# Merging the inverse blocks of a gated DeltaNet: products of four quadrants interleaved in PE's queue

## The chip, the cores and the metric

The kernel runs on one core of one Trainium2 chip. The metric is the device time of one execution in microseconds. The median of three runs shown of the kernel before is 1520.39 us (1517.37 to 1524.07).

## The reference, cut to what matters

One layer of a hybrid backbone: 256 context tokens and 1024 latent tokens of width 1024 pass a modulated RMSNorm, one wide input projection, two parallel groups of heads (a bidirectional gated DeltaNet with four heads of 128, and a bidirectional retention with rotary positions), an output projection, and a SwiGLU. All inputs and the output are float32. The change lies in the gated DeltaNet, in the triangular solve:

```python
kb = kc * bc[..., None]
A = jnp.where(strict, jnp.einsum('nbhid,nbhjd->nbhij', kb, kc) * decay, 0.0)
...
sol = lax.linalg.triangular_solve(A + jnp.eye(CHUNK, dtype=A.dtype), rhs,
                                  left_side=True, lower=True, unit_diagonal=True)
```

For every chunk, head and direction a unit triangular matrix I + A has to be inverted. The kernel works with chunks of 128 tokens, ten for the 1280 tokens, so there are 10 x 4 units for each of two directions. In the forward direction the stored (transposed) matrix is triangular one way, in the backward direction the other way.

## The kernel before, in words

**Where the time stands.** The kernel computes the modulated input `hhi`, `hlo` (each float32 value split in two halves for fast products), projects it group by group (`token_major`, `conv_block`), prepares and inverts the DeltaNet blocks (`pre`, `invert`, `merge`), scans both directions (`step`), runs the retention beside the scan (`backward`, `forward`), and ends with output projection and feed-forward part.

**The inverse.** `invert(b)` takes a batch of chunks (batches of four, four and two: 16, 16 and 8 units for each direction) and inverts the 32 x 32 diagonal blocks by forward substitution on DVE (lines 638 and 640, 31 steps of two operations). `merge(b)` builds the 128 x 128 inverses from them. It loads the matrices into `U` (one tile, [128, direction, chunk, head, 128]) and writes the inverted diagonal blocks over their places; `t64` holds the transposed inverted blocks. Both have one buffer, so the next batch's loads wait for the merge before to be done with them.

A merge has two levels. For a block-triangular matrix with diagonal inverses X and Y and off-diagonal block C, the off-diagonal block of the inverse is -X C Y. On the first level the blocks are 32 x 32, and there are four such places: two directions `d` times two halves `p`. Each place uses one quadrant `a` of 32 partitions and its neighbour `bb`; for direction 0 these are (0, 1) and (2, 3), for direction 1 they are (1, 0) and (3, 2). Before the change the code walks d, then p, and for each place:

- L679: for all units, a product with quadrant `a` as rows, into the partitions of `bb` of a PSUM bank;
- L681: DVE negates these 32 partitions into `xt1`;
- L683: for all units, the second product, rows `bb`, into the partitions of `a` of the same bank;
- L685: ACT copies them into `U`;
- L688 and L690, for p equal to d only: a third product, the transposed form that the second level needs, and its copy into `t64`.

On the second level the blocks are 64 x 64. For each direction, and for each group of eight units: L701 (product), L702 (negation of 64 partitions into `xt2`), L704 (second product), L705 (copy into `U`). L707 then writes each chunk of `U` to DRAM for the scan. Every product here is a float32 product, which the profile shows as two passes, each with a weight load of its own.

**PSUM.** `bank_b` draws from three banks of the tag `pb`. `pre` uses them too (`kk`, `qt`, `kq`), as do the scan steps of direction 0. The projections (`tm`) have three banks of their own, `pa`.

**What sets the order.** A planner goes through the program with a cost model, and issues at each point the instruction that is ready and stands earliest in the program, engine by engine; each engine then runs its queue in the planned order. So while a merge waits for DVE or ACT, the planner fills PE with products of later projections. In the stretch in question these are the groups of `token_major` that follow in the program: 8 and 9, then two scan steps for each direction, then 2 to 5 with rotary finish (`fin_rope`: DVE at L398 and L401, GpSimd at L403, the store at L391 from one of two `res` buffers). Their products are L381, L382 and L383; their weights are loaded and split by ACT (L319) and DVE (L320). When the projections are done, their memory goes to the retention, which then runs beside the remaining scan steps.

Of the kernel before, what the change touches and what calls it, by code (L numbers as in the profile page):

```python
# [17 lines left out]
P = 128  # L18
# [19 lines left out]
def build(nc, tc, ap, dbg=None, stop=None, marks=None):  # L38
    root = ExitStack()
    V, S, G, T, SY = nc.vector, nc.scalar, nc.gpsimd, nc.tensor, nc.sync  # L40

    def pool(name, bufs=1, side=None, space=None):
        kw = {}
        if side is not None:
            kw["side"] = side
        if space is not None:
            kw["space"] = space
        if space is not DRAM:
            kw["reuse_waits"] = "tile"
        es = ExitStack()  # L50
        p = es.enter_context(tc.tile_pool(name=name, bufs=bufs, **kw))
        root.push(es)
        p_close[id(p)] = es
        return p
# [10 lines left out]
    def checkpoint(name):  # L65
        if dbg is not None:
            marks.append((name, int(nc.cur_bb.bb.instructions[-1].name.split("-")[-1])))
        if stop == name:
            raise Stop()
# [16 lines left out]
    def bank(tag, name):  # L86
        return PS["pool"].tile([P, 512], F32, tag=tag, name=name, bufs=PS["tags"][tag])
# [4 lines left out]
    def bank_b(name):  # L92
        return bank("pb", name)
# [67 lines left out]
    try:  # L161
# [44 lines left out]
        for k in range(KT):  # L206
            for i in range(2):
                w = PA.tile([P, 1024], F32, tag="adaw", name="adaw", bufs=7)
# [3 lines left out]
                if k > last:  # L212

                    for j in range(8):
                        T.matmul(pst[:, 64 + 2 * j:66 + 2 * j], w[:, j * P:(j + 1) * P], csl[:, k, :],
                                 start=True, stop=True)
                    rows_of(0)
                    continue
                if 2 * k + i in PLAIN:

                    for j in range(2):
                        T.matmul(psr[2 * i + j][:2, :], csl[:, k, :], w[:, j * 512:(j + 1) * 512],
                                 start=False, stop=(k == last), **kw)
# [59 lines left out]
        for gi, grp in enumerate(XGROUPS):  # L283
            n, t0 = len(grp), grp[0]
# [8 lines left out]
            sl = slice(t0 * P, (t0 + n) * P)  # L293
# [158 lines left out]
        ps = bank_b("G")  # L452
# [14 lines left out]
        ps = bank_b("GT")  # L467
# [178 lines left out]
        def blocks(b):  # L646

            nu = len(BATCH[b]) * H
            nb = 4 * nu

            def blk(dram, k):
                return dram.rearrange("(u b) (i j) -> b i u j", b=4, j=32)[k]

            uu = GM.tile([P, 2, len(BATCH[b]), H, P], F32, tag="U", name="U%d" % b, bufs=1)
            SY.dma_start(uu.rearrange("p e c h j -> p e (c h) j"), un[b])
            tt = GM.tile([P, 2, nu, 64], F32, tag="t64", name="t64", bufs=1)
            G.memset(tt, 0.0)
            for k in range(4):
                SY.dma_start(uu[q32[k]].rearrange("p e c h j -> p (e c h) j")[:, :, q32[k]], blk(xds[b][:2 * nb], k))
                SY.dma_start(tt[q32[k]].rearrange("p e u j -> p (e u) j")[:, :, (k % 2) * 32:(k % 2) * 32 + 32],  # L660
                             blk(xds[b][2 * nb:], k))
            return uu, [uu[:, 1 - d] for d in range(2)], [tt[:, d] for d in range(2)]

        def merge(b):

            uu, ub, t64 = blocks(b)
            nu = len(BATCH[b]) * H
            q = q32
            for d in range(2):
                u = ub[d].rearrange("p c h j -> p (c h) j")  # L670
                t = t64[d]
                xt1 = GM.tile([P, 16, 32], F32, tag="xt1", name="xt1", bufs=1)
                for p in range(2):
                    a, bb = (2 * p, 2 * p + 1) if d == 0 else (2 * p + 1, 2 * p)
                    ps = bank_b("m1")
                    ca = (a % 2) * 32
                    v3 = lambda sl: ps[sl, :nu * 32].rearrange("p (n j) -> p n j", j=32)
                    for n in range(nu):
                        T.matmul(ps[q[bb], n * 32:n * 32 + 32], u[q[a], n, q[bb]], t[q[a], n, ca:ca + 32],  # L679
                                 start=True, stop=True)  # L680
                    V.tensor_scalar(xt1[q[bb], :nu, :], v3(q[bb]), -1.0, None, ALU.mult)  # L681
                    for n in range(nu):
                        T.matmul(ps[q[a], n * 32:n * 32 + 32], xt1[q[bb], n, :], u[q[bb], n, q[bb]],  # L683
                                 start=True, stop=True)
                    S.activation(u[q[a], :, q[bb]], v3(q[a]), AF.Copy)  # L685
                    if p == d:
                        for n in range(nu):
                            T.matmul(ps[q[bb], n * 32:n * 32 + 32], u[q[bb], n, q[bb]], xt1[q[bb], n, :],  # L688
                                     start=True, stop=True)
                        S.activation(t[q[bb], :, ca:ca + 32], v3(q[bb]), AF.Copy)  # L690
            for d in range(2):
                u = ub[d].rearrange("p c h j -> p (c h) j")
                t = t64[d]
                A = slice(0, 64) if d == 0 else slice(64, 128)
                B = slice(64, 128) if d == 0 else slice(0, 64)
                for n0 in range(0, nu, 8):
                    ps = bank_b("m2")
                    v3 = lambda sl: ps[sl].rearrange("p (n j) -> p n j", j=64)
                    xt2 = GM.tile([P, 8, 64], F32, tag="xt2", name="xt2", bufs=1)
                    for n in range(8):  # L700
                        T.matmul(ps[B, n * 64:n * 64 + 64], u[A, n0 + n, B], t[A, n0 + n, :], start=True, stop=True)  # L701
                    V.tensor_scalar(xt2[B], v3(B), -1.0, None, ALU.mult)  # L702
                    for n in range(8):
                        T.matmul(ps[A, n * 64:n * 64 + 64], xt2[B, n, :], u[B, n0 + n, B], start=True, stop=True)  # L704
                    S.activation(u[A, n0:n0 + 8, B], v3(A), AF.Copy)  # L705
            for c, t in enumerate(BATCH[b]):
                S.dma_start(sd[t, :, 2:8:5], uu[:, :, c].rearrange("p e h j -> p e (h j)"))  # L707
            checkpoint("mrg%d" % b)
# [10 lines left out]
        for h in range(H):  # L719
            y = newy()  # L720
            conv_block(8 + h, y, False)
            for t0, n in ((0, 2), (2, 4), (6, 4)):
                ps = bank_b("vT")
# [10 lines left out]
        GM = pool("gm")  # L734
        for t in BATCH[2]:
            pre(t)
        checkpoint("pre2")
        merge(0)
        SY.dma_start(rope, ap["rope"])
        invert(2)  # L740
        checkpoint("inv2")
        merge(1)
        merge(2)


# [350 lines left out]
        pairs = (0, 4, 1, 5, 2, 6, 3, 7)  # L1096
# [197 lines left out]
        w = {}  # L1294
# [198 lines left out]
```

## Time and profile before

| | |
|---|---|
| median of the runs shown | 1520.39 us |
| profiled execution | 1528.42 us, span 1526.6 us |
| mean granted TensorE clock | 0.971 |
| PE busy | 1441.8 us (94%), 8927 passes |
| DVE busy | 987.9 us (65%) |
| ACT busy | 607.7 us (40%) |
| GpSimd busy | 638.3 us (42%) |

PE is TensorE's matmul, PEld its weight load, DVE is VectorE, ACT is ScalarE, POOL is GpSimd. A busy PE need not be at its peak, since matmuls are pipelined and overlap: the time that a run of them takes is read from the distance of their starts. The granted clock is 1.00 at full speed and 0.50 when the chip halves TensorE's clock. The merges lie between 437 and 587 us of the span.

### The profile page before, as it was taken

How to read it: one execution, taken by the hardware profiler on the slowest of the kernel's cores; microseconds unless marked ns; L12 is line 12 of the kernel's file. 1: busy time of each engine (PE TensorE's matmuls, PEld its weight loads, DVE VectorE, ACT ScalarE, POOL GpSimd, SP SyncE). 2: the span in 40 equal slices, each digit the busy share in tenths (PEclk: the TensorE clock that was granted, in tenths of full speed). 3: DMA queues.
4: the chain of work that ended last, by engine and by line, in shares of the span. 5: the costliest groups of instructions: out<-in, count | busy, mean ns of one | idle time of the engine just before them, and what ended most of it. 6: DMA issues, size and time to landing. Idle time of an engine off the chain costs nothing.

```text
span 1526.6 us, 24250 instructions
## 1 busy us (share of the span) xinstructions
PE 1441.8 (94%) x8927; PEld 1245.5 (82%) x8927; DVE 987.9 (65%) x1940; ACT 607.7 (40%) x1267; POOL 638.3 (42%) x589
## 2 busy tenths in 40 slices
PE   6899999987999999999699899999999999999997
PEld 2898889976889999999578678877888888788886
DVE  5866795279766634678857778655655555558477
ACT  5633563375441111325544443223333333354445
POOL 0310101486123333324406659889755553226321
PEclk9899999998979999999999999999999999999999
DMA  8555784487683654995843346666422222685862
GB/s 329 187 169 170 204 248 148 145 256 237 175 253 105 223 172 166 336 405 211 279 147 125 120 138 203 239 226 221 147 104 105 105 103 92 211 291 193 291 219 111
DMA packets 171703, 298.16 MB, mean 195 GB/s; under 512 B 43368, under 2 KB 93752, under 8 KB 166208
## 3 DMA queue, kind: packets, MB, share of 16 engines
q1 hardware_dynamic: 119424, 251.07, 48.5%
q10 hardware_dynamic: 49360, 36.88, 7.9%
q0 software_dynamic: 2800, 8.65, 1.6%
q8 instruction: 70, 1.15, 0.3%
q14 instruction: 49, 0.40, 0.1%
HBM read 206.60 MB, written 89.96 MB: 194 GB/s over the span
## 4 chain that ended last, share of the span: by engine, by line
PE 65%; DVE 10%; DMA 9%; POOL 8%; issue 4%; ACT 3%; SPq 0%; ACTq 0%; POOLq 0%; DVEq 0%
PE ffn L1184 6%; PE ffn L1183 6%; PE ffn L1182 6%; PE fo L1308 5%; PE fo L1310 5%; PE fo L1309 5%; PE tm L383 4%; PE tm L382 4%; PE tm L381 4%; PE b L484 2%; PE b L486 2%; PE b L485 2%; DMA wd<-tw 2%; DMA adaw<-ada_w 1%; PE op L1043 1%
## 5 line engine op out<-in xcount | busy, mean ns | idle before, releaser
L381 PE MATMUL tm<-whi,hhi 128*128 128x256 f32 (+1 forms) x704 | 205.8, 296 | 9.6 <-ACT hhi L278 4.7
L382 PE MATMUL tm<-wlo,hhi 128*128 128x256 f32 (+1 forms) x704 | 207.0, 295 | 3.7 <-DVE wlo L320 3.7
L383 PE MATMUL tm<-whi,hlo 128*128 128x256 f32 (+1 forms) x704 | 206.9, 297 | 0.5 <-DVE hlo L281 0.5
L381 PEld LDWEIGHTS tm<-whi,hhi 128*128 128x128 f32 x704 | 139.5, 199 | 12.0 <-ACT whi L319 5.5
L382 PEld LDWEIGHTS tm<-wlo,hhi 128*128 128x128 f32 x704 | 140.6, 200 | 6.7 <-DVE wlo L320 4.4
L383 PEld LDWEIGHTS tm<-whi,hlo 128*128 128x128 f32 x704 | 139.9, 200 | 3.2 <-issue 0.9
L1182 PE MATMUL ffn<-t,whi 128*128 128x512 f32 x352 | 137.2, 391 | 4.3 <-ACT whi L319 3.2
L1184 PE MATMUL ffn<-t,wlo 128*128 128x512 f32 x352 | 137.1, 390 | 1.6 <-DVE wlo L320 1.6
L1183 PE MATMUL ffn<-t,whi 128*128 128x512 f32 x352 | 137.1, 389 | 0.5 <-DVE t L1077 0.5
L320 DVE TENSOR_TENSOR wlo<-ws,whi 128x512 fp32r<-128x512 f32 x88 | 94.3, 1072 | 51.3 <-ACT whi L319 51.0
L320 DVE TENSOR_TENSOR wlo<-wraw,whi 128x512 fp32r<-128x512 f32 (+2 forms) x92 | 101.0, 1099 | 38.3 <-ACT whi L319 38.0
L319 ACT ACTIVATE whi<-wraw 128x512 fp32r<-128x512 f32 (+2 forms) x98 | 75.2, 772 | 123.6 <-PE ffn L1183 80.0
L319 ACT ACTIVATE whi<-ws 128x512 fp32r<-128x512 f32 x88 | 55.6, 631 | 171.8 <-PE ffn L1183 117.5
L1308 PE MATMUL fo<-whi,ahi 128*128 128x512 f32 x308 | 119.3, 389 | 0.7 <-ACT ahi L319 0.7
L1309 PE MATMUL fo<-wlo,ahi 128*128 128x512 f32 x308 | 119.9, 389 | 0.0
L1310 PE MATMUL fo<-whi,alo 128*128 128x512 f32 x308 | 119.0, 389 | 0.0
L1182 PE MATMUL ffn<-b,whi 128*128 128x512 f32 x264 | 103.7, 393 | 3.9 <-ACT whi L319 3.9
L1184 PE MATMUL ffn<-b,wlo 128*128 128x512 f32 x264 | 103.9, 394 | 2.1 <-DVE wlo L320 2.1
L1183 PE MATMUL ffn<-b,whi 128*128 128x512 f32 x264 | 103.5, 392 | 0.0
L484 PE MATMUL b<-hhi,whi 128*128 128x512 f32 (+1 forms) x256 | 95.1, 372 | 2.0 <-ACT y L488 1.9
L485 PE MATMUL b<-hlo,whi 128*128 128x512 f32 (+1 forms) x256 | 94.8, 370 | 0.0
L486 PE MATMUL b<-hhi,wlo 128*128 128x512 f32 (+1 forms) x256 | 94.4, 369 | 0.0
(422 smaller groups left out, 3566.5 us busy)
## 6 DMA issues: line engine op xcount, KB each, us to landing
adaw<-ada_w SPq DMA_DIRECT2D x48, 512.0 KB, 5.7
pk<-sd SPq DMA_DIRECT2D x16, 1536.0 KB, 9.2
wraw<-wfi SPq DMA_DIRECT2D x44, 512.0 KB, 3.5
ar<-ad SPq DMA_DIRECT2D x33, 512.0 KB, 5.7
w<-wfo SPq DMA_DIRECT2D x22, 512.0 KB, 3.6
wd<-tw SPq DMA_DIRECT2D x11, 1024.0 KB, 5.1
ad<-act SPq DMA_DIRECT2D x20, 512.0 KB, 4.2
raw<-wd SPq DMA_DIRECT2D x20, 512.0 KB, 5.2
```

The costliest lines, as they stand in the source:

```text
L319: S.activation(hi, raw, AF.Copy)
L320: e.tensor_tensor(lo, raw, hi.bitcast(F32), ALU.subtract)
L381: T.matmul(o, hhi[:, k, tsl], whi[:, k % 4, :], start=(k == 0), stop=False)
L382: T.matmul(o, hhi[:, k, tsl], wlo[:, k % 4, :], start=False, stop=False)
L383: T.matmul(o, hlo[:, k, tsl], whi[:, k % 4, :], start=False, stop=(k == KT - 1))
L484: T.matmul(o, whi[:, k, :], hh, start=(k == 0), stop=False)
L1182: T.matmul(o, whi[:, k, :], xhi(xn, slice(0, 4), k), start=(first and k == 0), stop=False, **kw)
L1183: T.matmul(o, whi[:, k, :], xlo(xn, slice(0, 4), k), start=False, stop=False, **kw)
L1184: T.matmul(o, wlo[:, k, :], xhi(xn, slice(0, 4), k), start=False, stop=(k == 3), **kw)
L1308: T.matmul(po[g][i], ahi[:, ts], whi, start=(j == 0 and not kw), stop=False, **kw)
L1309: T.matmul(po[g][i], ahi[:, ts], wlo, start=False, stop=False, **kw)
L1310: T.matmul(po[g][i], alo[:, ts], whi, start=False, stop=(j == FH - 1), **kw)
```

## The change

The loops over direction and half move inside the loop over units. For the first level, all units and all four places are first multiplied into one bank (`ps1`), in the order unit 0 place 1, 2, 3, 4, unit 1 place 1 and so on; one DVE instruction over all 128 partitions negates them into `xt1`; then the second and third products of all units and places follow, interleaved in the same way, into two further banks (`ps2`, `ps3`); then come the six ACT copies. On the second level, for each group of eight units, both directions are interleaved in the same manner, with one negation over 128 partitions and two banks. The products themselves, their number and their operands, the copies by ACT, the loads and the stores are the same as before. DVE's negations go from twelve and ten to three and five.

```diff
-            for d in range(2):
-                u = ub[d].rearrange("p c h j -> p (c h) j")
-                t = t64[d]
-                xt1 = GM.tile([P, 16, 32], F32, tag="xt1", name="xt1", bufs=1)
-                for p in range(2):
-                    a, bb = (2 * p, 2 * p + 1) if d == 0 else (2 * p + 1, 2 * p)
-                    ps = bank_b("m1")
...
-                    for n in range(nu):
-                        T.matmul(ps[q[bb], n * 32:n * 32 + 32], u[q[a], n, q[bb]], t[q[a], n, ca:ca + 32],
+            pairs = [(d, p) + ((2 * p, 2 * p + 1) if d == 0 else (2 * p + 1, 2 * p)) for p in range(2) for d in range(2)]
+            three = lambda ps, sl, w: ps[sl].rearrange("p (n j) -> p n j", j=w)
+            ps1 = bank_b("m1")
+            for n in range(nu):
+                for d, p, a, bb in pairs:
                     ca = (a % 2) * 32
+                    T.matmul(ps1[q[bb], n * 32:n * 32 + 32], u[d][q[a], n, q[bb]], t[d][q[a], n, ca:ca + 32],
+                             start=True, stop=True)
+            xt1 = GM.tile([P, 16, 32], F32, tag="xt1", name="xt1", bufs=1)
+            V.tensor_scalar(xt1.rearrange("p n j -> p (n j)")[:, :nu * 32], ps1[:, :nu * 32], -1.0, None, ALU.mult)
+            ps2, ps3 = bank_b("m1"), bank_b("m1")
+            for n in range(nu):
+                for d, p, a, bb in pairs:
+                    T.matmul(ps2[q[a], n * 32:n * 32 + 32], xt1[q[bb], n, :], u[d][q[bb], n, q[bb]],
+                             start=True, stop=True)
+                    if p == d:
+                        T.matmul(ps3[q[bb], n * 32:n * 32 + 32], u[d][q[bb], n, q[bb]], xt1[q[bb], n, :],
                                  start=True, stop=True)
...
+            for d, p, a, bb in pairs:
+                S.activation(u[d][q[a], :, q[bb]], three(ps2[:, :nu * 32], q[a], 32), AF.Copy)
+                if p == d:
+                    ca = (a % 2) * 32
+                    S.activation(t[d][q[bb], :, ca:ca + 32], three(ps3[:, :nu * 32], q[bb], 32), AF.Copy)
+            halves = [(0, slice(0, 64), slice(64, 128)), (1, slice(64, 128), slice(0, 64))]
+            for n0 in range(0, nu, 8):
+                ps1, ps2 = bank_b("m2"), bank_b("m2")
+                xt2 = GM.tile([P, 8, 64], F32, tag="xt2", name="xt2", bufs=1)
+                for n in range(8):
+                    for d, A, B in halves:
+                        T.matmul(ps1[B, n * 64:n * 64 + 64], u[d][A, n0 + n, B], t[d][A, n0 + n, :], start=True, stop=True)
+                V.tensor_scalar(xt2.rearrange("p n j -> p (n j)"), ps1, -1.0, None, ALU.mult)
+                for n in range(8):
+                    for d, A, B in halves:
+                        T.matmul(ps2[A, n * 64:n * 64 + 64], xt2[B, n, :], u[d][B, n0 + n, B], start=True, stop=True)
+                for d, A, B in halves:
+                    S.activation(u[d][A, n0:n0 + 8, B], three(ps2, A, 64), AF.Copy)
```

More of the change, by code (lines that the diff above doesn't have):

```diff
@@ L668, in merge @@
             q = q32
-            for d in range(2):
-                u = ub[d].rearrange("p c h j -> p (c h) j")
-                t = t64[d]
-                xt1 = GM.tile([P, 16, 32], F32, tag="xt1", name="xt1", bufs=1)
-                for p in range(2):
-                    a, bb = (2 * p, 2 * p + 1) if d == 0 else (2 * p + 1, 2 * p)
-                    ps = bank_b("m1")
-                    ca = (a % 2) * 32
-                    v3 = lambda sl: ps[sl, :nu * 32].rearrange("p (n j) -> p n j", j=32)
-                    for n in range(nu):
-                        T.matmul(ps[q[bb], n * 32:n * 32 + 32], u[q[a], n, q[bb]], t[q[a], n, ca:ca + 32],
-                                 start=True, stop=True)
[L681 to L705, printed above, removed]
+            u = [x.rearrange("p c h j -> p (c h) j") for x in ub]
@@ new lines, in merge @@
+            t = t64
+            pairs = [(d, p) + ((2 * p, 2 * p + 1) if d == 0 else (2 * p + 1, 2 * p)) for p in range(2) for d in range(2)]
[3 more added lines that the diff above has]
+                for d, p, a, bb in pairs:
+                    ca = (a % 2) * 32
+                    T.matmul(ps1[q[bb], n * 32:n * 32 + 32], u[d][q[a], n, q[bb]], t[d][q[a], n, ca:ca + 32],
+                             start=True, stop=True)
```

## The prediction

> **What bounds the kernel now.** I read the page's busy line first, then the same engines cut into stretches around the merges, then the merge products (tile m) alone.
>
> ```profile
> PE 1441.8 (94%) x8927; PEld 1245.5 (82%) x8927; DVE 987.9 (65%) x1940; ACT 607.7 (40%) x1267; POOL 638.3 (42%) x589
> ...
> 437.00:587.00 150.00, 147.36 (x1804) 141.21 (x1805) 74.39 (x189) 25.74 (x40) 44.74 (x84) 0.89 0.56 166
> 587.00:616.00 29.00, 29.00 (x252) 29.00 (x251) 13.61 (x44) 3.50 (x6) 9.28 (x20) 1.00 0.72 272
> 616.00:725.00 109.00, 106.47 (x936) 105.16 (x936) 84.12 (x317) 42.95 (x123) 38.59 (x40) 1.00 0.83 312
> 725.00:763.00 38.00, 25.06 (x173) 22.43 (x172) 31.78 (x106) 19.82 (x56) 15.28 (x15) 0.91 0.83 280
> ...
> 437.00:587.00 150.00, 52.92 (x1120) 49.08 (x1120) 14.06 (x22) 15.07 (x28) 0.00 (x0) 0.89 0.56 166
> ```
>
> In a stretch the columns are length, busy of PE, PEld, DVE, ACT and POOL, granted clock, DMA share and GB/s. All three merges lie between 437 and 587 us. PE is busy for 147.4 of those 150 us, while DVE has half its time free and ACT most of it. The last row is the merges' own share: 52.9 us of PE in 1120 passes (each f32 product is two passes), 22 DVE and 28 ACT instructions. The rest of PE there is the token-major projection (tile tm), which the planner pours in between. PE stays full to 725 us; only then does a stage bounded by latencies begin. So what the merges give back of PE's time is first filled with later tm work, and everything up to 725 us can move forward. That is the claim on which the forecast rests.
>
> **The merge products: price now.** From the chain of waits (start, length) and the lists by line:
>
> ```profile
> 505.88 2.95 PE m L679 x96
> 513.97 2.04 PE m L683 x64
> 478.56 2.00 PE m L701 x32
> ...
> L679 PE MATMUL m<-t,U x320: 190/191/258, 437.7 to 570.1; 32*32 32x32 f32 x160
> L683 PE MATMUL m<-U,xt x320: 191/191/258, 448.1 to 574.1; 32*32 32x32 f32 x160
> L688 PE MATMUL m<-xt,U x160: 191/191/257, 454.0 to 578.2; 32*32 32x32 f32 x160
> L701 PE MATMUL m<-t,U x160: 218/218/312, 463.7 to 582.0; 64*64 64x64 f32 x160
> L704 PE MATMUL m<-U,xt x160: 218/218/268, 470.3 to 586.3; 64*64 64x64 f32 x160
> ```
>
> A pass takes 191 or 218 ns from start to end but these pipeline: 2.95 us / 96 = 30.7 ns per 32-row pass, 2.00 / 32 = 62.5 ns per 64-row pass. There are 800 of the first (320 + 320 + 160) and 320 of the second: 24.6 + 20.0 = 44.6 us. The 8.3 us missing to 52.9 are passes at half clock and drains.
>
> **Edit 1, products of the quadrants interleaved unit by unit.** No product is added or taken away; their order changes, so that neighbours in PE's queue use different 32-row (64-row) strips and write different partitions. Before, that happens only where one run of products ends and another begins. Such places in PE's timeline (start, length):
>
> ```profile
> 462.54 0.21 PE L679 MATMUL m<-t,U 32*32 32x32 f32 x1
> 462.56 0.19 PE L683 MATMUL m<-U,xt 32*32 32x32 f32 x1
> 462.59 0.19 PE L679 MATMUL m<-t,U 32*32 32x32 f32 x1
> 462.60 0.19 PE L683 MATMUL m<-U,xt 32*32 32x32 f32 x1
> ...
> 471.17 0.22 PE L701 MATMUL m<-t,U 64*64 64x64 f32 x1
> 471.18 0.22 PE L704 MATMUL m<-U,xt 64*64 64x64 f32 x1
> 471.23 0.22 PE L701 MATMUL m<-t,U 64*64 64x64 f32 x1
> 471.24 0.22 PE L704 MATMUL m<-U,xt 64*64 64x64 f32 x1
> ```
>
> Each run keeps its own cadence, and the two run side by side: four starts in 0.06 us at 32 rows, two starts every 0.06 us at 64 rows. Two streams thus cost about 16 ns and 30 ns a pass. The change has two streams at 64 rows and four at 32. Four are shown nowhere; bounds are 30.7 ns (no overlap) and 30.7 / 4 = 8 ns; I take 12, between the shown 16 and 8. Then 800 x 12 + 320 x 30 = 9.6 + 9.6 = 19.2 us against 52.9: a gain of **33.7 us**, bounds 0 and 52.9 - 6.4 - 9.6 = 37.
>
> The Trainium skill (TensorE: Matmul & The Clock Gate, section "Wait — 56ns, not 53.3ns?") says that starts never come closer than about 25 ns however small the product. The rows above disagree, with four starts in 0.06 us; by the rule 800 x 25 + 9.6 = 29.6 us would be left, a gain of 23.
>
> **Edit 2, fewer and longer bursts.** Entering and leaving a burst costs something beside its passes:
>
> ```profile
> 478.05 0.28 PE L381 MATMUL tm<-whi,hhi 128*128 128x256 f32 x1
> 478.17 0.28 PE L382 MATMUL tm<-wlo,hhi 128*128 128x256 f32 x1
> 478.28 0.28 PE L383 MATMUL tm<-whi,hlo 128*128 128x256 f32 x1
> 478.49 2.08 PE L701 MATMUL m<-t,U 64*64 64x64 f32 x32
> 480.50 0.39 PE L381 MATMUL tm<-whi,hhi 128*128 128x256 f32 x1
> 480.72 0.28 PE L382 MATMUL tm<-wlo,hhi 128*128 128x256 f32 x1
> ```
>
> A tm pass follows the one before by 0.12 us; into the burst it is 0.21, after it 0.22: 0.2 us a burst. The code's product loops go from 50 (12 + 12 + 6 + 10 + 10) to 16 (two per merge, two per group of eight units); many of the 50 already adjoin. Between 0 and 34 x 0.2 = 7 us; I take **2 us**.
>
> **Edit 3, the clock.**
>
> ```profile
> 437.40:461.30 23.90, 13.48 (x58) 12.60 (x59) 1.22 (x4) 0.74 (x2) 0.50 0.80 211
> ...
> 505.80:509.00 3.20, 3.20 (x99) 3.15 (x99) 3.07 (x9) 0.00 (x0) 0.98 (x2) 1.00 0.90 217
> 509.20:512.60 3.40, 3.40 (x18) 3.40 (x17) 3.08 (x9) 0.00 (x0) 1.36 (x3) 0.51 0.11 39
> 516.00:519.40 3.40, 3.40 (x47) 3.27 (x47) 2.20 (x9) 0.59 (x1) 0.48 (x2) 1.00 0.11 39
> ...
> 440.06 0.41 PE L381 MATMUL tm<-whi,hhi 128*128 128x256 f32 x1
> 440.27 0.41 PE L382 MATMUL tm<-wlo,hhi 128*128 128x256 f32 x1
> ```
>
> The first row counts tm passes alone; its clock column is 0.50 for 23.9 us. There 58 passes went at 0.21 us rather than 0.12, 5 us lost. The burst of 2.95 us at 505.88 was followed by a stretch at 0.51; that of 2.04 us at 513.97 was not (clock 1.00). So long runs of small products cost clock. With 12 ns the longest new burst (a merge's second and third products, 192 passes) lasts 2.3 us, below that mark, and the first merge's half-clock stretch should end sooner. Bounds: +5 us, or a loss (rival D); I take **+2 us**.
>
> **Edit 4, evacuation.**
>
> ```profile
> L685 ACT ACTIVATE U<-m 32x512 f32<-32x512 f32 (+1 forms) x12 | 6.2, 517 | 57.1 <-PE m L683 57.0
> ```
>
> L681 and L702, together 22 DVE instructions busy 14.06 us, become three negations over all partitions and five for the second level. ACT keeps its 28, but six of them now stand in a row behind the whole second batch. Both are off the path: ACT has 124 of 150 us free, DVE 76. Without cover the ACT run would cost 6 x 0.52 = 3 us per merge. Queued behind ACT's wait are the weight splits (L319) for the next tm group, behind DVE's the rope operations (L398, L401) and the inverse of the third batch (L638, L640); PE waits for each, but all have slack now. PSUM: a merge's ps1, ps2 and ps3 are all three banks of their tag, shared with the preparation of the third batch, whose products end before the merge, and with the first scan steps, which come after. I put **0** for the whole, bounds -5 and +5. Blocks of the next merge load sooner, since U has one buffer; SP's queue then takes them earlier, at a DMA share of 0.56. They hide behind tm.
>
> **What is late next.** The freed time is used by rope tiles, and those pass through two res buffers (first row: min/median/max ns, first and last start; the rows with a bar: busy us, mean ns, idle before them and its cause; last row: us to landing):
>
> ```profile
> L398 DVE TENSOR_TENSOR ra<-tm,rope x36: 401/424/427, 456.7 to 620.4; 128x256 f32<-128x256 f32 x36
> ...
> L401 DVE TENSOR_TENSOR res<-tm,rope 128x128 f32<-128x128 f32 x56 | 13.6, 279 | 5.8 <-DMA rd<-res 5.7
> L403 POOL TENSOR_TENSOR res<-ra,res 128x128 f32<-128x128 f32 x56 | 27.1, 501 | 95.4 <-DVE res L401 95.4
> L391 POOL DMA_DIRECT2D rd<-res x28 | 15.8, 565 | 8.3 <-POOL res L403 7.4 <-DMA rd<-res 0.9
> DMA to landing us min/median/max: 2.2/3.7/7.8
> ```
>
> A buffer is held for about 2 x 0.28 (L401) + 2 x 0.50 + 0.57 + 3.7 = 5.8 us, so a tile can leave every 2.9 us, or every 4.9 where the landing takes 7.8. Now 36 tiles start in 456.7 to 620.4 us, 4.7 us apart; with 37.7 us less it is 3.6. That is above 2.9 but below 4.9, so slow landings will show: 1.3 us for perhaps five or six of 36. I take **7 us** back (bounds 0 and 20).
>
> **Sum.** 33.7 + 2 + 2 + 0 - 7 = 31 us. The profiled execution took 1528.4 us (span 1526.6), so it would become 1497; it stands 8.0 us above the median of the runs shown, 1520.4, which becomes **1489**.
>
> **The rivals.**
> B, overlap at 64 rows alone. Four 32-row streams crowd PE's queue and a pass there stays near 30 ns, so only the 64-row level gains: 24.0 + 9.6 = 33.6, gain 19, less some 3 for res: 1504. For it: the trace shows only two streams overlapping, and only for a few passes. Against: those passes came 16 ns apart on average.
>
> C, no overlap within one bank. All neighbours that overlapped in the trace wrote different banks, since each run had its own; the change puts them all in one. If PE serializes writers of a bank, 52.9 us stay and only the bursts' 2 us go: 1518, no change. Against: the partitions written are distinct. The Trainium skill (TensorEngine Tiling (Array Packing), section "Gotcha 1: PSUM Pressure") says that different row tiles can't access the same PSUM bank simultaneously; no row of this trace can confirm it.
>
> D, slower, by the clock. If a pass costs over 2.95 us / 192 = 15.4 ns, the second batch of a merge is a longer burst than the one after which the clock fell. At 30.7 ns it is 5.9 us, and each merge may fall into a half-clock stretch like the 23.9 us now seen once: two more of these cost 2 x 23.9 / 2 = 24 us, less some 8 where merges are already slowed, less 2 for bursts: 1520 + 14 = 1534. It needs C's serialization (or the planner setting batches back to back).
>
> E, absorbed. PE is freed, but res buffers or the DMA of the scan (0.83 share in 616 to 725 us) hold the end: 1520 - 5 = 1515.
>
> **How the numbers follow.** A, the forecast, 0.50 (own range 1474 to 1500); B 0.15; C 0.12; E 0.08; D 0.15. About 0.5%, 7.6 us, is what a measurement can tell from no change. Faster: A, B and the part of C and E that gains more than that, 0.67; same: the rest of C and E, 0.18; slower: D, 0.15. The range reaches from 1470 (8 ns a pass, clock gained, nothing given back) to 1526, which takes in C and E and the mild end of D.
>
> **What would show it.** Edit 1: merge products alone below 25 us of PE busy, starts of four lines' worth within 32 ns; B about 34, C over 45. Edit 3: granted clock in the merges' stretch above 0.89 for A, lower for D. Next limit: waits of L401 on rd<-res above the present 5.7 us. If tile m falls to 20 us and the end of tm does not come 25 us or more before 616 us, the step that fails is that PE alone held this stretch.

## The result, and the profile after

The median went from 1522.23 us (1517.37 to 1525.78, four runs) to **1499.95 us** (1497.97 to 1501.01, four runs): 22.3 us less, a ratio of **0.986 [0.983, 0.989]**. The forecast was 1489, its range 1470 to 1526. The profiled execution went from 1528.42 to 1499.94 us, by 28.5.

The page's busy line of the kernel after:

```profile
PE 1405.7 (94%) x8927; PEld 1210.8 (81%) x8927; DVE 978.5 (65%) x1926; ACT 607.0 (41%) x1267; POOL 638.6 (43%) x589
```

PE has the same 8927 passes and is busy 36.1 us less. To see where, the profile is cut in both kernels from the first merge product to the last token-major one. The rows that give these ends (by line: min/median/max ns, first and last start), of after:

```profile
L679 PE MATMUL m<-t,U x320: 184/194/258, 434.7 to 532.7; 32*32 32x32 f32 x160
L383 PE MATMUL tm<-whi,hlo x294: 274/282/582, 430.0 to 587.0; 128*128 128x256 f32 x147
L1185 PE MATMUL ffn<-b,whi x264: 389/389/793, 844.5 to 1282.7; 128*128 128x512 f32 x132
```

and two of before:

```profile
L383 PE MATMUL tm<-whi,hlo x301: 274/281/582, 429.9 to 617.0; 128*128 128x256 f32 x151
L1182 PE MATMUL ffn<-b,whi x264: 389/389/628, 873.5 to 1312.1; 128*128 128x512 f32 x132
```

The diff moves line numbers: L683, L688, L701 and L704 of before are L686, L689, L702 and L706 of after. The last token-major product comes 30.0 us earlier (617.0 to 587.0), the first feed-forward product 29.0 (873.5 to 844.5). The stretch itself in windows (length, then busy time and count of PE, PEld, DVE, ACT and POOL, granted clock, DMA share, GB/s), first everything, then tile m alone, then tile tm alone. Before:

```profile
437.70:617.20 179.50, 177.52 (x2064) 171.33 (x2065) 87.30 (x232) 28.54 (x45) 53.62 (x103) 0.91 0.58 184
437.70:617.20 179.50, 52.88 (x1120) 49.01 (x1120) 14.06 (x22) 15.23 (x28) 0.00 (x0) 0.91 0.58 184
437.70:617.20 179.50, 121.31 (x863) 113.91 (x863) 29.11 (x103) 0.74 (x2) 0.91 0.58 184
```

After:

```profile
434.70:587.20 152.50, 141.56 (x2068) 136.84 (x2069) 79.34 (x220) 28.75 (x45) 55.23 (x107) 0.95 0.70 217
434.70:587.20 152.50, 22.83 (x1120) 19.85 (x1120) 5.23 (x8) 14.90 (x28) 0.00 (x0) 0.95 0.70 217
434.70:587.20 152.50, 113.74 (x863) 108.15 (x863) 29.78 (x105) 0.77 (x2) 0.95 0.70 217
```

Both hold the same 1120 merge passes and 863 token-major passes, so this is a ledger of the 27.0 us by which the stretch is shorter:

| us of PE | before | after | difference |
|---|---|---|---|
| merge products (tile m) | 52.9 | 22.8 | -30.1 |
| token-major products (tile tm) | 121.3 | 113.7 | -7.6 |
| other products (scan), the rest of busy | 3.3 | 5.0 | +1.7 |
| idle (length less busy) | 2.0 | 10.9 | +9.0 |
| length | 179.5 | 152.5 | -27.0 |

The merges gave back 30 us, and the token-major passes, the same in number, another 7.6; 9 us of this came back as waits, which PE had hardly had before. What the new waits are (engine, line, what it waited for: us in all, times, longest), before and after in the same stretch:

```profile
PE tm L382 <- DVE wlo L320: 1.9, 2, 1.2
PE m L679 <- DMA t<-xd: 0.7, 1, 0.7
```

```profile
PE m L679 <- issue: 3.4, 1, 3.4
PE m L689 <- DMA U<-xd: 2.8, 1, 2.8
PE m L686 <- issue: 2.5, 2, 1.7
PE tm L382 <- DVE wlo L320: 1.0, 2, 0.8
```

8.7 us of the waits after stand at merge products, the longest of each kind in the second merge. The chain of waits (start, length) shows what they wait for:

```profile
465.33 5.24 DMA sd<-U
470.69 10.05 DMA U<-un
...
481.71 2.52 SPq L659
484.27 7.49 DMA U<-xd
491.81 0.35 PE m L686 x19
```

The first merge's last chunk is stored from `U` until 470.6; only then can the single `U` be loaded again (10.05 us, until 480.7); the inverted diagonal blocks are written over it until 491.8. The first product of the second merge started at 480.83, 0.1 us behind the end of that load, the first that needed the last diagonal block at 491.81. PE reached both points ahead of the data. The list calls the first of these waits `issue`, a wait for nothing that the profile shows; that it was for the load is read from the times. For the other `issue` wait of the second merge (1.7 us, ended at 495.35) no such cause is shown.

### The profile page after: what moved, and what is told of

Read it like the earlier page. It is cut to its first block, busy times and chain, and to the rows that moved or that the text cites. A ratio compares the mean times of both kernels' runs of the same rounds, so it can differ in the third digit from the quotient of the medians.

```text
span 1498.2 us, 24215 instructions
## 1 busy us (share of the span) xinstructions
PE 1405.7 (94%) x8927; PEld 1210.8 (81%) x8927; DVE 978.5 (65%) x1926; ACT 607.0 (41%) x1267; POOL 638.6 (43%) x589
## 3 DMA queue, kind: packets, MB, share of 16 engines
q8 instruction: 70, 1.15, 0.3%
## 4 chain that ended last, share of the span: by engine, by line
PE 64%; DVE 12%; DMA 10%; POOL 5%; issue 4%; ACT 3%; SPq 1%; ACTq 0%; POOLq 0%; DVEq 0%
PE ffn L1187 8%; PE ffn L1186 8%; PE ffn L1185 8%; PE tm L383 4%; PE tm L382 4%; PE tm L381 4%; PE fo L1313 3%; PE fo L1312 3%; PE fo L1311 3%; PE b L484 2%; PE b L486 2%; PE b L485 2%; PE op L1044 2%; PE op L1046 2%; PE op L1045 2%
## 5 line engine op out<-in xcount | busy, mean ns | idle before, releaser
L381 PE MATMUL tm<-whi,hhi 128*128 128x256 f32 (+1 forms) x704 | 203.9, 292 | 8.7 <-ACT whi L319 4.3
L383 PE MATMUL tm<-whi,hlo 128*128 128x256 f32 (+1 forms) x704 | 204.4, 293 | 0.0
L381 PEld LDWEIGHTS tm<-whi,hhi 128*128 128x128 f32 x704 | 137.4, 196 | 11.1 <-ACT whi L319 5.4
L383 PEld LDWEIGHTS tm<-whi,hlo 128*128 128x128 f32 x704 | 137.6, 196 | 2.2 <-issue 0.9
L319 ACT ACTIVATE whi<-wraw 128x512 fp32r<-128x512 f32 (+2 forms) x98 | 75.2, 772 | 132.0 <-PE ffn L1186 77.6
L319 ACT ACTIVATE whi<-ws 128x512 fp32r<-128x512 f32 x88 | 55.6, 631 | 170.6 <-PE ffn L1186 120.1
```

The source lines that it names most:

```text
L319: S.activation(hi, raw, AF.Copy)
L381: T.matmul(o, hhi[:, k, tsl], whi[:, k % 4, :], start=(k == 0), stop=False)
L383: T.matmul(o, hlo[:, k, tsl], whi[:, k % 4, :], start=False, stop=(k == KT - 1))
```

## The experiments

Theory O says that the gain is the overlap of neighbouring products in PE's queue, passed to the end one for one, less new waits. Rivals put it to the fewer and longer bursts or the single negation, or say that something other than PE holds the stretch; W and R are two readings of what holds it after the change: W the loads of the second merge (the expectation of e10 calls this one L), R the two `res` buffers of the rope tiles.

First a reading that all of them need. The profiled executions, in three parts of the span: until the first merge product, from there to the first feed-forward product, and from there to the end (cut by first starts; us). The first and the third part run the same work in every kernel.

| kernel | tile m busy | until first m | first m to last tm | **first m to first ffn** | behind | median |
|---|---|---|---|---|---|---|
| before | 52.9 | 437.7 | 179.3 | **435.8** | 653.0 | 1522.2 |
| before again | 52.4 | 436.7 | 179.2 | **436.2** | 652.1 | one run |
| after | 22.9 | 434.7 | 152.4 | **409.8** | 653.7 | 1500.0 |
| e1 not interleaved | 42.3 | 432.7 | 168.7 | **426.5** | 651.0 | 1514.7 |
| e2 first level only | 29.6 | 435.5 | 157.5 | **416.8** | 653.3 | 1509.8 |
| e3 second level only | 36.0 | 434.3 | 163.4 | **420.3** | 647.7 | 1502.3 |
| e4 four negations | 24.9 | 437.5 | 158.5 | **417.0** | 648.8 | 1502.5 |
| e6 before, doubled | 86.1 | 437.4 | 214.3 | **473.2** | 649.4 | 1556.1 |
| e7 places reordered | 21.8 | 437.4 | 159.1 | **417.1** | 651.5 | 1506.6 |
| e8 second merge later | 22.7 | 435.0 | 148.7 | **409.4** | 646.2 | 1499.5 |
| e10 three res buffers | 21.8 | 440.3 | 149.4 | **406.8** | 648.7 | 1494.7 |
| e11 both | 21.3 | 437.9 | 141.2 | **410.5** | 647.3 | 1502.8 |
| e12 two streams | 26.0 | 435.0 | 160.3 | **420.4** | 651.9 | 1507.5 |

The outer parts differ by up to 7.6 us (432.7 to 440.3, and 646.2 to 653.7), although the last one has exactly 2780 passes in each and no edit touches it (of the first part, e10's 440.3 is a case of its own, see there). Here the last one is in before, after, e2 and e3, one window row each:

```profile
873.60:1526.60 653.00, 635.39 (x2780) 521.69 (x2780) 408.10 (x525) 245.82 (x438) 366.05 (x247) 0.99 0.51 175
```

```profile
844.50:1498.20 653.70, 636.57 (x2780) 522.68 (x2780) 406.38 (x525) 245.67 (x438) 366.00 (x247) 0.99 0.50 175
```

```profile
852.30:1505.60 653.30, 637.75 (x2780) 523.31 (x2780) 404.40 (x525) 245.94 (x438) 366.06 (x247) 0.99 0.51 175
```

```profile
854.60:1502.30 647.70, 635.22 (x2780) 523.67 (x2780) 409.03 (x525) 246.11 (x438) 366.65 (x247) 0.99 0.51 177
```

PE's work there is the same to within 2.5 us; its idle time is 17.6, 17.1, 15.6 and 12.5 us. So a difference of 5 us between the medians of two plans need not come from the merges. The column in bold is the better witness for them, though each of its entries is one execution; before's two agree within 0.4.

**e9, the kernel before once more** (no edit).

> The kernel before, unchanged, for a second profile: how far do the clock's stretches and the end of the token-major work (617.0 us in the first profile, an execution 6 us above the median of before) move between executions. Theory O: the plan is fixed, only the clock moves; the end of tm falls at 608 to 615 us.

1526.77 us, tile m 52.4 us. The half-clock stretch of 23.9 us at the start of the merges came again, at 437.5 us: it belongs to this kernel's order and is not an accident of one execution. The last token-major product started at 615.9 us, just outside the 608 to 615 expected.

**e1, not interleaved**: the change, with places outside and units inside again, on both levels; banks, bursts, negations and copies stay those of the change.

```diff
-            for n in range(nu):
-                for d, p, a, bb in pairs:
+            for d, p, a, bb in pairs:
+                for n in range(nu):
...
-                for n in range(8):
-                    for d, A, B in halves:
+                for d, A, B in halves:
+                    for n in range(8):
```

(each of the two at both product loops of its level)

> The changed kernel with the unit loop put back inside the loop over places (and over directions on the second level): the same bursts, banks, negations and copies, but neighbours in PE's queue again use the same strip. Theory O (overlap of the strips is the gain): a pass costs 30.7 and 62.5 ns again, so 800 x (30.7 - 9) + 320 x (62.5 - 30) = 28 us of PE come back, and all of the gain with them: 1520 to 1530 us. Rival S (the gain is from fewer bursts, one negation for four and the earlier end of each merge): it stays at 1500 to 1506. Rival K (clock: longer bursts without overlap drop the clock): over 1530.

1514.73 us (1511.99 to 1518.1), ratio 0.995 [0.992, 0.997]: two thirds of the gain are gone; the theory had expected all of it to go, 1520 to 1530. The timeline (start, length) shows why. Of e1, four rows near the start of the first merge's second batch, the third merge's first products, and one 64-row run, each of the last two followed by eight passes out of its middle:

```profile
446.36 0.19 PE L686 MATMUL m<-U,xt 32*32 32x32 f32 x1
446.37 0.19 PE L689 MATMUL m<-xt,U 32*32 32x32 f32 x1
446.39 0.19 PE L686 MATMUL m<-U,xt 32*32 32x32 f32 x1
446.40 0.19 PE L689 MATMUL m<-xt,U 32*32 32x32 f32 x1
...
541.06 1.91 PE L679 MATMUL m<-t,U 32*32 32x32 f32 x64
541.15 0.41 PE L679 MATMUL m<-t,U 32*32 32x32 f32 x8
...
555.92 1.90 PE L706 MATMUL m<-U,xt 64*64 64x64 f32 x32
556.09 0.63 PE L706 MATMUL m<-U,xt 64*64 64x64 f32 x8
```

Less the last pass's own 0.19 us, 64 passes in 1.91 us are 27 ns each on the average. This run has four pieces of 16 passes, one for each place, and it is quicker where one piece passes into the next, on another strip. Inside a piece a pass costs 31 ns ((0.41 less 0.19) / 7), and at 64 rows 59 ((0.63 less 0.22) / 7): on one strip there is no overlap of these products. But the second and the third product of a place, which before stood in two loops (L683, L688), stand side by side in the change's second loop, and there the starts are 0.015 us apart. They read the same 32-row strip and write different partitions (of different banks, `ps2` and `ps3`), and they overlap all the same. So e1 had not undone the whole overlap; tile m stands at 42.3 us, not at 52.9, and the bold column shows 9.3 us of gain for these 10.6. This overlap makes about 5 of the 10.6, an estimate from 160 passes of third products at 31 ns. The rest no run separates; the fewer bursts of rival S may have a share in it.

**e2 and e3, one level alone**: e2 undoes the lower half of that diff's edits (64-row products not interleaved), e3 the upper half (32-row products not interleaved).

> The changed kernel with only the 32-row products interleaved; on the second level the loop over directions is outside the loop over units. Theory O: 320 x (62.5 - 30) = 10 us of PE come back: 1510 us. Rival S: 1500 to 1503.

> The changed kernel with only the 64-row products interleaved; on the first level the loop over places is outside the loop over units. Theory O: 800 x (30.7 - 9) = 17 us of PE come back: 1517 us; together with the run where only the first level is interleaved the losses add up to that of the run with neither. Rival S: 1500 to 1503. Rival K: bursts of 192 passes last 5.9 us and drop the clock, over 1522.

e2: 1509.78 (1505.36 to 1515.68), ratio 0.993 [0.990, 0.995], as theory O expected. e3: 1502.25 (1499.9 to 1504.11), ratio 0.987 [0.985, 0.989], some 15 us below theory O's 1517 and inside rival S's band. By the medians the second level alone would give nearly everything; by the merges' own stretch it is the other way round: 19.0 us for the first level alone, 15.5 for the second alone, 26.0 for both. In the two profiled executions, 1507.39 us of e2 and 1504.11 of e3, the part behind the merges, which neither edit touches, is 5.6 us shorter in e3 (the rows above), while the merges' stretch is 3.5 us longer. Whether this also holds for the executions at the medians is not shown. The parts don't add up (19.0 + 15.5 = 34.5), and can't: e1 shows that 9.3 us come with the new loops even where nothing else is interleaved, and both contain these. Less them it is 9.7 + 6.2 + 9.3 = 25.2 against 26.0.

**e12, two streams**: on the first level two places at a time, the other two after them.

```diff
-            for n in range(nu):
-                for d, p, a, bb in pairs:
+            for n, (d, p, a, bb) in [(n, pr) for h in range(2) for n in range(nu) for pr in pairs[2 * h:2 * h + 2]]:
+                if True:
```

> The changed kernel with the first level interleaved two places at a time (both directions of one half, then of the other) instead of four. Theory O with the price set by the strip's own cadence: 31 / 2 = 15.5 ns a pass for the first products at full clock, against 8.6 with four and 29 with one; merge products busy 26 us, 1500 to 1508 us. Rival (two streams already reach PE's issue limit): 9 ns.

1507.48 us (1503.05 to 1509.89), ratio 0.990 [0.986, 0.993]; tile m 26.0: both as expected. The same 64 passes of the third merge, beside e1's row above; first e12, then after, with the 128 of the second merge and one 64-row run:

```profile
529.33 1.11 PE L679 MATMUL m<-t,U 32*32 32x32 f32 x64 [1.97 <-POOL res L403]
```

```profile
532.14 0.75 PE L679 MATMUL m<-t,U 32*32 32x32 f32 x64
480.83 1.28 PE L679 MATMUL m<-t,U 32*32 32x32 f32 x128 [3.38 <-issue]
546.54 1.15 PE L706 MATMUL m<-U,xt 64*64 64x64 f32 x32
```

In the same reckoning a pass costs **15 ns with two streams and 9 with four** ((1.11, 0.75 less 0.19) / 63), where one strip alone costs 31 and e1's run of four pieces 27; at 64 rows it costs 30 with two streams ((1.15 less 0.22) / 31), where one costs 59. Each strip nearly keeps its own cadence (31, 2 x 15, 4 x 9), and all four write one PSUM bank. This is theory O at its smallest scale, and it falsifies a serialization by the bank for writers of different partitions. The stretch of e12 is 10.6 us longer than after's for 3.1 us of merge products; token-major passes take 3.0 of the rest (116.7 against 113.7), and what is left is not traced to the edit.

**e7, other order of the places**: 0, 2, 1, 3 in place of 0, 1, 2, 3.

```diff
-... for p in range(2) for d in range(2)]
+... for d in range(2) for p in range(2)]
```

> The changed kernel with the four places in the order direction outside, half inside: strips 0, 2, 1, 3 instead of 0, 1, 2, 3. Any order keeps four strips as neighbours. Theory O: the same 8 to 10 ns a pass, 1497 to 1504 us. Rival P (the planner's order decides the result, and any edit moves it by more than 8 us): outside of 1493 to 1507.

1506.64 us (1504.9 to 1509.02), ratio 0.989 [0.986, 0.992]; tile m 21.8, the same as after. The products don't care about the order of the strips. The median is 2.6 us above the narrow band expected, and the stretch 7.3 us longer: PE idled more in it, at merge products (`U<-xd` 4.1 us), a weight split (3.3) and a rope tile (2.6). Another plan, other waits.

**e4, four negations**: the change with a negation for each quadrant and for each half.

```diff
-            V.tensor_scalar(xt1.rearrange("p n j -> p (n j)")[:, :nu * 32], ps1[:, :nu * 32], -1.0, None, ALU.mult)
+            for k in range(4):
+                V.tensor_scalar(xt1[q[k]].rearrange("p n j -> p (n j)")[:, :nu * 32], ps1[q[k], :nu * 32], -1.0, None, ALU.mult)
...
-                V.tensor_scalar(xt2.rearrange("p n j -> p (n j)"), ps1, -1.0, None, ALU.mult)
+                for d, A, B in halves:
+                    V.tensor_scalar(xt2[B].rearrange("p n j -> p (n j)"), ps1[B], -1.0, None, ALU.mult)
```

> The changed kernel with the negations cut up again: four DVE instructions of 32 partitions on the first level and two of 64 on the second instead of one over all 128. 14 more DVE instructions of 0.4 to 0.7 us, some 9 us of DVE. Theory O (PE's overlap is the gain, DVE has slack): 1497 to 1504 us. Rival N (the single negation is part of the gain): 1506 or more.

1502.48 us (1499.52 to 1505.14), ratio 0.986 [0.983, 0.989], the change's own and inside the 1497 to 1504 expected. Tile m by windows in e4 (DVE is the third busy column):

```profile
430.00:590.00 160.00, 24.87 (x1120) 21.41 (x1120) 14.07 (x22) 15.03 (x28) 0.00 (x0) 0.94 0.69 216
```

DVE has all its 22 negations and 14.1 us back, and the time is the same. In the profile the stretch is 7.2 us longer, of which 2.8 are token-major passes (116.55 against 113.74) and 2.0 merge products; with one execution for each this is no more than a hint that the single negation has some worth.

**e6, the kernel before with its first products issued twice** (L679 and L701; the second product writes the same values to the same place).

```diff
-                    for n in range(nu):
+                    for n in [n for n in range(nu) for _ in range(2)]:
...
-                    for n in range(8):
+                    for n in [n for n in range(8) for _ in range(2)]:
```

> The kernel before with each first product of both levels (L679 and L701) issued twice, the second overwriting the first with the same values: 320 x 30.7 + 160 x 62.5 = 19.8 us more of PE between 437 and 587 us, nothing else. Theory O with PE as what holds this stretch: 1522 + 18 to 24 = 1540 to 1546 us. Rival E (the end is held by the res buffers, the loads or the scan, and PE time there is worth little): less than 1532.

1556.1 us (1555.96 to 1561.74), ratio 1.023 [1.021, 1.026]: 34 us more, not 18 to 24. Tile m and everything by windows, and one burst:

```profile
437.40:651.90 214.50, 213.44 (x2569) 207.04 (x2569) 89.76 (x248) 29.97 (x46) 54.58 (x107) 0.84 0.47 152
437.40:651.90 214.50, 86.06 (x1600) 81.96 (x1600) 14.04 (x22) 15.21 (x28) 0.00 (x0) 0.84 0.47 152
...
442.37 4.81 PE L679 MATMUL m<-t,U 32*32 32x32 f32 x126 [0.31 <-DVE ut L603]
```

The 480 added passes cost 33.2 us of PE (86.06 less 52.88), 69 ns each, because the clock fell from 0.91 to 0.84 in the stretch: 569 merge passes ran at half clock, 196 before. And the stretch grew by 35.0 us (179.5 to 214.5). So what PE gets to do there reaches the end one for one, and these long runs of small products did cost clock; the size of the latter had been missed.

**e8, the second merge later**: its first products wait for the fourth tile of group 3 (`last_tm[3, 3]`), and groups 8, 9, 2 and 3 stand ahead of the second and third merge in the program, so that token-major work fills PE while `U` is loaded.

```diff
+                    last_tm[g, t] = T.matmul(o, hlo[:, k, tsl], whi[:, k % 4, :], start=False, stop=(k == KT - 1)).ins
...
+            with tc.issue_after(last_tm[3, 3]) if b == 1 else nullcontext():
+                for n in range(nu):
...
+        for g in (8, 9):
+            token_major(g, LAT, fin_gate, S, W)
+        for g in (2, 3):
+            token_major(g, ALL, fin_rope, G, W)
         merge(1)
         merge(2)
```

> The changed kernel with the second merge's first products held back in PE's queue behind two more tiles of token-major work (some 70 passes, 8.4 us), because in the changed kernel PE stood for 3.4 us ahead of that merge and for 2.8 and 2.5 us within it, waiting for its blocks to load. Theory W (these waits are what was lost of the freed time): the waits go, 1491 to 1496 us. Rival F (the wait is refilled later or the end is held elsewhere): 1498 to 1502.

**e10, a third res buffer**, and **e11, both**.

```diff
-                res = (W2 if early else R1).tile([P, 256], F32, tag="res", name="res", bufs=4 if early else 2)
+                res = (W2 if early else R1).tile([P, 256], F32, tag="res", name="res", bufs=4 if early else 3)
```

> The changed kernel with three res buffers for the rotary tiles instead of two. Theory R (as the prediction had it: the two res buffers hold back the freed time): DVE's wait of L401 on stores, 7.0 us, falls below 3, PE's gaps in the stretch fall, 1493 to 1497 us. Theory L (the second merge's loads, which stand one after the other behind the first merge's store in the chain of waits, hold it): 1498 to 1503.

> The second merge held back by two tiles of token-major work and three res buffers together. If both limits take turns (each alone only shows the other), the two together give what neither gives alone: PE's gaps fall from some 10 us to under 5 and the time to 1490 to 1494 us. If the give-back has other causes: 1497 to 1502.

e8: 1499.46 us (1492.37 to 1503.87), ratio 0.985 [0.981, 0.989], no change against after, which is rival F's case. Its second merge begins at 509.5 us, not at 480.8, and yet PE idles 10.1 us between the first merge product and the last token-major one, against 10.9 in after. e10: **1494.70** (1492.53 to 1500.0), ratio 0.982 [0.979, 0.985], the lowest of all and inside theory R's 1493 to 1497. e11: 1502.81 (1497.45 to 1505.15), ratio 0.987 [0.984, 0.989], above both ranges expected. L401, the rope operation that writes `res`, in groups (busy us, mean ns, idle before and its cause), after and e10:

```profile
L401 DVE TENSOR_TENSOR res<-tm,rope 128x128 f32<-128x128 f32 x72 | 17.2, 280 | 11.4 <-DMA rd<-res 7.0 <-DMA zd<-res 4.3
```

```profile
L401 DVE TENSOR_TENSOR res<-tm,rope 128x128 f32<-128x128 f32 x70 | 16.7, 278 | 0.0
```

PE's longest wait then between 425 and 600 us, in e10 and in e11 (whose L383 is the L381 of the others), and one of e11 behind 590 us:

```profile
PE tm L381 <- ACT whi L319: 8.8, 1, 8.8
```

```profile
PE tm L383 <- ACT whi L319: 8.4, 1, 8.4
...
PE yT L1031 <- DMA yt<-dy: 4.0, 1, 4.0
```

The third buffer takes L401's wait away whole. The waits of 8.8 and 8.4 us for a weight split (in e10 from 430.9 us on) stand ahead of the first merge product; no kernel with two buffers waits more than 2.8 us there for L319, ACT's half of such a split. In the stretch itself PE idles 9.1 us in e10 and 6.8 in e11, against 10.9 in after, where e11 was to come under 5. The stretch to the feed-forward part is 3.0 us shorter than after's, the part behind it 5.0, the part ahead 5.6 longer. R's time came true, but the gaps that it was to close hardly closed: neither W nor R is shown to hold the 9 us. Moving the merge (e8) takes 3.7 us off the stretch to the last token-major product, both edits (e11) take 11.2, and by the first feed-forward product this is given back: e11 has 269.4 us from 579.0 to its first feed-forward product, all the others 256.5 to 260.7. Among what it has there and after has not is the 4.0 us for `yt<-dy`. Each wait that was taken away left room for another. e10 beats both kernels by its median, but its interval overlaps the change's, so that its lead over after stays unproved.

## Why the prediction was right, and where its sizes were off

**PE alone holds the stretch: right.** The mark set was a last token-major product 25 us or more earlier; it was 30.0. e6, in the other direction, gave 35.0 us of stretch for 33.2 of PE. With this rival E fell, in which other limits absorb the freed time.

**Edit 1, overlap: right in mechanism, 3.6 us too good.** Tile m is at 22.8 us, below the mark of 25; predicted 19.2. A 32-row pass at full clock costs 9 ns (12 was taken, 8 the bound), a 64-row pass 30 as predicted. At these prices 800 x 9 + 320 x 30 makes 16.8; the remaining 6 us are what the step left out, the last pass's own 0.2 us at the end of each burst (18 unbroken runs in PE's order), and passes at half clock. Of the old 52.9 us the prediction had put 8.3 down to these two and let them go to nothing without a reason. One further source was not seen: the second and the third product of a place overlap even without interleaving the places (e1).

**Rivals B and C fell.** Four strips overlap nearly as fully as two, and in one bank: 31, 15 and 9 ns. The Trainium skill's statement that different row tiles can't access the same PSUM bank simultaneously (TensorEngine Tiling (Array Packing), section "Gotcha 1: PSUM Pressure") does not hold here for writers of different partitions; nor does the floor of about 25 ns between starts (TensorE: Matmul & The Clock Gate, section "Wait — 56ns, not 53.3ns?"), with 128 passes in 1.28 us on four strips; on one strip starts stay 31 ns apart. D needed a pass to stay above 15.4 ns, and it did not.

**Edit 2, bursts: open.** No run isolates the 2 us; e1 has the new bursts, but also the second overlap. In PE's order the merge products stand in 25 unbroken runs before and 18 after; at the prediction's 0.2 us each this gives an estimate of 1.4 us.

**Edit 3, clock: right in sign, too small.** The 863 token-major passes of the stretch take 7.6 us less, where 2 was taken and 5 was the bound; not all of it need be the clock. Windows of after at half clock:

```profile
434.30:441.10 6.80, 5.80 (x141) 5.04 (x142) 5.45 (x14) 4.17 (x5) 0.46 (x1) 0.50 1.11 222
482.10:485.50 3.40, 3.40 (x17) 3.40 (x17) 3.30 (x8) 0.00 (x0) 2.82 (x5) 0.50 1.16 235
492.30:499.10 6.80, 5.09 (x153) 4.89 (x142) 2.50 (x11) 3.32 (x6) 0.73 (x2) 0.50 0.08 24
```

These are 17.0 us in all; before had 34.1 in its stretch, 23.9 of them in the one that the prediction quoted. The token-major passes alone, summed over the half-clock windows of the stretch, before and after:

```profile
sum 34.20, PE 23.11 PEld 22.23 DVE 2.47 ACT 0.74; mean PE 5.78 PEld 5.56 DVE 0.62 ACT 0.18
sum 16.70, PE 10.43 PEld 9.90 DVE 1.29 ACT 0.38; mean PE 3.48 PEld 3.30 DVE 0.43 ACT 0.13
```

12.7 us less of them ran at half clock. As a pass takes 0.12 us at full clock and 0.21 at half, this is worth between 5 and 6 us by estimate; the rest of the 7.6 may be edit 2's. Rival D's mechanism shows in e6. That shorter runs are what raised the clock here is not shown: e1, with runs of up to 4.6 us, has 24.0 us at half clock, less than before.

**Edit 4, evacuation and negations: right.** Nothing, by e4's median, for the negations. The six copies in a row and the three banks no run isolates.

**What is late next: the size nearly, the place wrong.** 7 us were taken, 9.0 came. L401's wait for `rd<-res`, the sign that the prediction named, did not rise. Its 5.7 us come from a window that ends at 590 us, where the rope tiles of before go on to 617; over the whole stretch of before the row is

```profile
L401 DVE TENSOR_TENSOR res<-tm,rope 128x128 f32<-128x128 f32 x68 | 16.5, 280 | 8.2 <-DMA rd<-res 8.1
```

against 7.0 us after (and 6.0 in before again), with 4.3 for `zd<-res` new beside it. PE's list for after has no wait behind L401; PE waits in the second merge for `U`. The sentence that failed is that the next merge's blocks "hide behind tm": with PE 25 us ahead (the second merge starts at 480.83, before at 505.88), store, load and overlay through one `U` end after PE gets there. What the runs then show is less simple than either: with either wait moved, another takes its place.

**The sum and the forecast.** In the profiled executions 31 us were forecast and 28.5 came. That they lie so close is in part luck: the merge products gave 3.6 us less than was taken, edits 2 and 3 together 3.6 more (7.6 for 4), waits and other products took 3.7 more, and 1.5 came from outside the stretch. The 11 us between 1489 and 1500 lie mostly in the last step, which took before's distance of profile and median (8.0 us) over to the new kernel. After's profiled execution stands at its own median. Before's runs scatter widely, from 1512.39 to 1528.94 in the batch beside e4, the first at a mean granted clock of 0.980, the last at 0.970; after's four lie within 3.0 us. The gain should have been taken as a share of an execution at the median, with less half-clock time to win back; this is argued, as both profiles of before lie above its median.

## What to carry to other kernels

Where a full PE runs many small independent products, put neighbours into its queue that use different row strips: time falls with the number of streams, within one bank too if they write different partitions. Doubling the small products in a row cost clock as well (e6). Before counting the freed time as won, ask of each single-buffered tile on the new path whether its store and reload still end before PE arrives. And where later parts of a kernel scatter by several microseconds with unchanged work, judge an edit by the stretch that it touches beside the medians.

## What the runs showed of the hardware that was not expected

- 32-row float32 passes on one strip start 31 ns apart; in two streams a pass costs 15 ns and in four 9, in one PSUM bank. 128 passes, each with its own weight load, took 1.28 us.
- Two products that read the same 32-row strip overlap too, if they write different partitions: starts 0.015 us apart in e1. They also wrote different banks; whether one bank would do, no run shows.
- After's short runs of small products did not keep the clock up where PE had just been idle: the 1.28 us burst at 480.83 stood behind 3.38 us of idle time, and half clock followed at 482.1, though the 2.04 us burst of before had none behind it. e7's burst of 1.28 us behind 2.6 us of idle time was followed by half clock too, e2's behind 1.2 us was not. That idle time and small products count alike fits these rows; no run tested it alone.
- Not all small products cost clock alike. In e1 a run of 64 passes of 64 rows (L706, then L702) took 3.58 us from 461.76 on, and the clock stayed full; a run of 128 passes of 32 rows took 3.95 us from 486.4 on, and half clock followed. The windows:

```profile
456.20:490.00 33.80, 32.59 (x429) 31.76 (x429) 27.45 (x71) 4.49 (x6) 15.41 (x28) 1.00 0.61 187
490.10:493.50 3.40, 3.40 (x21) 3.34 (x19) 2.93 (x8) 0.00 (x0) 0.45 (x1) 0.50 1.21 284
```

- The last 2780 passes of the span, the same in every kernel, took 646.2 to 653.7 us at a mean clock of 0.99. Whether a kernel keeps its place in this scatter is open; before's two profiles gave 653.0 and 652.1.
